# Linear attention scores in three visits of 32x32 matmul tiles instead of seven, from packed copies of K and Q

## The chip, the core and the metric

One core of a Trainium2 chip runs the whole program. The metric is device time in microseconds (us) of that core, the median of several executions of the same program. TensorE (PE) does the matmuls, and its weight loads have a row of their own (PEld); VectorE (DVE) and ScalarE (ACT) work on tiles element by element and can read PSUM, GpSimd (POOL) works element by element on SBUF, and SyncE (SP) issues most DMAs. Each engine runs its own instructions in program order, and engines wait for each other by semaphores.

## The reference, cut to what matters

The program is one layer of a hybrid model: an input projection whose columns feed a gated linear recurrence (group A, 16 column blocks) and an HGRN2 linear attention (group B, 16 heads of 128 channels), then an output projection. There are 512 latent tokens (T) behind 256 context tokens (C), 768 in all (TA). The change concerns the scores of the linear attention:

```python
F = jnp.cumsum(gc, axis=2)
diff = F[:, :, :, None, :] - F[:, :, None, :, :]
decay = jnp.exp(jnp.where(causal[:, :, None], diff, -jnp.inf))
scores = jnp.einsum('bhtk,bhsk,bhtsk->bhts', qc, kc, decay)
o = jnp.einsum('bhts,bhsv->bhtv', scores, vc) + jnp.einsum('bhtk,bhkv->bhtv', qc * jnp.exp(F), s)
```

Every pair of a query t and a key s in a chunk is weighted by the product of the forget factors f between them, channel by channel, forwards and backwards in time. The kernel uses chunks of 128 tokens. In such a chunk the pairs are split by the highest bit in which t and s differ: the diagonal (t = s), and seven levels l = 0 to 6, level l holding the pairs in neighbouring blocks of m = 2^l tokens. At each level K and Q already carry the decay to the edges of their blocks, so that a plain matmul gives the scores of that level.

## The kernel before, in words

The program first computes norms and modulations, then walks the input projection column block by column block. A column block is a *unit*. A unit takes four *slots* (`g` = 0 to 3); in a slot, PE does four K steps of projection matmuls. Each step has three matmuls (high part by high part, high by low, low by high; `mm_unit`) of 512 columns (L177), or of 256 and of 512 columns where the context is needed too (L174, L175). So a slot has 12 matmuls in a unit without context (q and gb), and 24 in a unit with it (ff, v, fb). At the start of each slot ACT rounds the weights for a later slot to a high part `whi` (L127), and POOL subtracts to get the low part `wlo` (L128).

The units of a head come in the order q, gb, ff, v, fb. When fb is done, ACT takes sigmoids, DVE makes the forget factors T (L553) and the keys K (L554), and `steps_b(h)` puts the head's attention work as a list of steps into a queue `wq`. `run_steps` takes steps from it: one at the end of each slot, and one more in the middle of the slot where the next step is marked *fast*. In this way the steps of head h stand, on every engine, between the projection slots of head h+1: the slots of its q and gb units hold `prep` and `level(0)` to `level(6)`, those of ff hold the transposes `ktr` (L526, two of them in a slot) and then the state matmuls `umm` (L654), and so on to `fin`. For the last head, h = 15, the next slots are those of the output projection's first quarter (`q == 0`; 12 matmuls of 512 columns at L826 in each `kb`), where one step runs ahead of each `kb`'s matmuls and where DVE and ACT also split the input y into parts (`y_conv`, L717 and L718).

`prep` packs K into `Kc` on ACT (L563), adds the two directions' K into `kd` (L571) and makes the decayed queries Q (L574, L575). `level(l)` has a PE part and a DVE part. On PE it is a *visit*: 16 matmuls of 32x32 tiles (L581), with 16 more for the diagonal at l = 0 and eight of 64x64 (L609) at l = 6. On DVE it decays K (L613) and Q (L617) to the next block size, merges T (L619), and takes the scores out of PSUM: under a mask into `mc` (copy_predicated, L622) for l < 5, into `mg` for l = 5 and 6 (L631, L635, with ACT's L630 and L634). ACT packs K for the next level after each decay of K (L563), into one of two buffers. The moving operand Q is read in place, in strides.

Among the steps DVE also has the products of the q and gb units (L534, which wait for ACT's sigmoid `sg`, L532) and one accumulation of the output gate in each unit (`gate_step`, L499), until 64 of those are done, which is in head 12. After every 16th of them a step `go` (L506 to L509) is put into the queue, which moves the steps behind it by one slot.

## Time and profile before

| what | before |
| --- | --- |
| median of 3 runs | 2338.56 us (2337.93 to 2340.09) |
| span of the profiled execution | 2338.6 us |
| PE busy | 2254.7 us (96%) |
| DVE busy | 1414.9 us (61%) |
| POOL busy | 931.5 us (40%) |
| ACT busy | 883.7 us (38%) |
| L581, visits of 32x32 tiles: matmuls recorded (two for each of the program's) | 3584 (2560 + 512 + 512) |
| L613, decay of K on DVE | 112, 1579 ns each on average |

The profiled execution has no time of its own beside its span, which is that of the median. Busy times are sums over the whole program, and an engine at 61% may be full in one stage and empty in another; what a stage is bound by is read from the stage. A wait is put down to the engine whose semaphore came last.

### The profile page before, as it was taken

Reading aid. Unit: us, or ns where it says so; the run is one execution under the profiler, and the core shown is the slowest. Engines: PE = TensorE matmul, PEld = TensorE weight load, DVE = VectorE, ACT = ScalarE, POOL = GpSimd, SP = SyncE. Lnnn points to the kernel's source line nnn. Section 1 sums busy time; section 2 is a strip of 40 time slices with the busy share of each in tenths; the row PEclk is TensorE's granted clock in tenths of the full one; section 3 lists DMA queues with packets and bytes.
Section 4 is the critical chain, followed back from the end, with each engine's and each line's share of the span. In section 5 each row is a group of like instructions: output and inputs, shape, how many; then the busy total and the mean of one; then the engine's idle time right before and its main releaser. Section 6 shows DMA issues by size and latency. Waiting matters only on the chain.

```text
span 2338.6 us, 38901 instructions
## 1 busy us (share of the span) xinstructions
PE 2254.7 (96%) x15520; PEld 1863.1 (80%) x15520; DVE 1414.9 (61%) x2223; ACT 883.7 (38%) x1604; POOL 931.5 (40%) x682
## 2 busy tenths in 40 slices
PE   5999999999999999999999999999999998999998
PEld 3568888888888788888788888878878887788886
DVE  4446666666657867766776785686776577720011
ACT  4237677766722232332232222223223223432222
POOL 1225565555533333433333332333333233355552
PEclk9999999999999999999999999999999999999999
DMA  9952222222222222222222232222222123553443
GB/s 342 316 183 78 76 87 82 81 70 93 77 73 77 91 79 84 84 82 84 80 77 86 74 96 77 75 90 82 82 82 77 65 64 105 159 179 95 123 125 108
DMA packets 119086, 241.95 MB, mean 103 GB/s; under 512 B 13556, under 2 KB 13940, under 8 KB 118904
## 3 DMA queue, kind: packets, MB, share of 16 engines
q1 hardware_dynamic: 116216, 231.06, 31.2%
q0 software_dynamic: 2688, 8.40, 0.9%
q8 instruction: 122, 2.00, 0.3%
q14 instruction: 60, 0.49, 0.1%
HBM read 226.81 MB, written 12.59 MB: 102 GB/s over the span
## 4 chain that ended last, share of the span: by engine, by line
PE 61%; DVE 20%; issue 5%; ACT 4%; POOL 1%; ACTq 0%; POOLq 0%; DVEq 0%
PE m L175 22%; PE m L174 11%; PE m L177 8%; PE w L826 8%; PE m L826 6%; DVE ktok L526 5%; DVE KK L613 4%; DVE QQ L617 3%; PE w L654 2%; PE w L352 1%; DVE T L619 1%; DVE mg L631 1%; PE w L351 1%; DVE KK L554 1%; DVE gacc L499 1%
## 5 line engine op out<-in xcount | busy, mean ns | idle before, releaser
L128 POOL TENSOR_TENSOR wlo<-wraw,whi 128x512 fp32r<-128x512 f32 x556 | 784.3, 1415 | 1140.9 <-ACT whi L127 1072.5
L175 PE MATMUL m<-h,whi 128*128 128x512 f32 x1984 | 738.5, 395 | 0.0
L174 PE MATMUL m<-h,whi 128*128 128x256 f32 x1984 | 563.1, 284 | 1.5 <-ACT xp L303 1.5
L127 ACT CAST whi<-wraw 128x512 fp32r<-128x512 f32 x556 | 342.2, 620 | 551.6 <-PE m L175 181.0
L177 PE MATMUL m<-h,whi 128*128 128x512 f32 x1440 | 456.0, 398 | 0.0
L175 PEld LDWEIGHTS m<-h,whi 128*128 128x128 f32 x1984 | 372.3, 188 | 82.6 <-issue 0.7
L175 PE MATMUL m<-h,wlo 128*128 128x512 f32 x992 | 391.1, 394 | 0.0
L174 PEld LDWEIGHTS m<-h,whi 128*128 128x128 f32 x1984 | 375.0, 189 | 4.3 <-ACT xp L303 1.9
L177 PEld LDWEIGHTS m<-h,whi 128*128 128x128 f32 x1440 | 263.4, 188 | 55.0 <-issue 0.5
L177 PE MATMUL m<-h,wlo 128*128 128x512 f32 x720 | 281.3, 391 | 0.0
L174 PE MATMUL m<-h,wlo 128*128 128x256 f32 x992 | 279.0, 281 | 0.0
L175 PEld LDWEIGHTS m<-h,wlo 128*128 128x128 f32 x992 | 186.0, 187 | 44.9
L174 PEld LDWEIGHTS m<-h,wlo 128*128 128x128 f32 x992 | 187.3, 189 | 0.0
L613 DVE TENSOR_TENSOR KK<-KK,T 128x768 f32<-128x768 f32 x112 | 176.8, 1579 | 2.7 <-PE w L609 1.8
L177 PEld LDWEIGHTS m<-h,wlo 128*128 128x128 f32 x720 | 135.2, 188 | 29.8
L320 DVE SCALAR_TENSOR_TENSOR u<-xp,P,u 128x256 f32<-128x256 f32 x96 | 86.5, 960 | 114.4 <-ACT u L318 114.4
L526 DVE STREAM_TRANSPOSE ktok<-KK 32x384 f32<-32x384 f32 x256 | 145.7, 569 | 3.3
L563 ACT COPY Kc<-KK 128x512 f32<-128x512 f32 x80 | 54.8, 684 | 176.2 <-DVE KK L613 119.8
L617 DVE TENSOR_TENSOR QQ<-QQ,T 128x512 f32<-128x512 f32 x112 | 115.3, 1030 | 0.4 <-PE w L581 0.2
L526 DVE STREAM_TRANSPOSE vtok<-ktok 32x192 f32<-32x192 f32 x256 | 94.6, 370 | 13.1 <-ACT ktok L539 9.9
L826 PE MATMUL m<-whi,yh 128*128 128x512 f32 x256 | 102.0, 399 | 0.0
L826 PE MATMUL m<-wlo,yh 128*128 128x512 f32 x256 | 101.2, 395 | 0.0
(209 smaller groups left out, 3068.1 us busy)
## 6 DMA issues: line engine op xcount, KB each, us to landing
wraw<-in_wi SPq DMA_DIRECT2D x428, 256.0 KB, 3.2
araw<-in_adas SPq DMA_DIRECT2D x64, 512.0 KB, 6.1
wraw<-in_wo SPq DMA_DIRECT2D x128, 256.0 KB, 2.6
wraw<-in_adag SPq DMA_DIRECT2D x64, 256.0 KB, 2.7
y_d<-ys POOLq DMA_DIRECT2D x32, 256.0 KB, 2.4
wraw<-y_d SPq DMA_DIRECT2D x32, 256.0 KB, 2.8
h<-in_xT SPq DMA_DIRECT2D x16, 384.0 KB, 7.5
w0raw<-in_w SPq DMA_DIRECT2D x16, 320.0 KB, 6.6
```

The costliest lines, as they stand in the source:

```text
L127: act.copy(hi, t)
L128: pool.tensor_sub(lo, t, hi.bitcast(F32))
L174: pe.matmul(ph[:, 0, 0:C], w, h[:, 0:C], start=s, stop=e)
L175: pe.matmul(ph[:, 1, :], w, h[:, C:TA], start=s, stop=e)
L177: pe.matmul(ph, w, h[:, C:TA], start=s, stop=e)
L320: dve.scalar_tensor_tensor(dst, xp[:, o + k:o + k + n], cw, dst, op0=ALU.mult, op1=ALU.add)
L526: dve.transpose(dst[32 * j:32 * j + 32, :, 32 * i:32 * i + 32], src[32 * i:32 * i + 32, :, 32 * j:32 * j + 32])
L563: act.copy(kc.rearrange("p c n -> p (c n)").rearrange("p (a b c) -> p a b c", b=2, c=m), view(s["K"], C, [[2 * m, C // m], [TA + m, 2], [1 ...
L613: dve.tensor_mul(kk, kk, view(Tm, 1, [[2, nb // 2], [nb - 1, 2], [0, m]]))
L617: dve.tensor_mul(qq, qq, view(Tm, nb + 1 + C // m, [[2, C // m], [-nb - 1, 2], [0, m]]))
L654: pe.matmul(pw[:, i, :], s["kt"][:, 6 * tl[o + i][0] + tl[o + i][1], :], s["v"][:, tl[o + i][1], :], start=True, stop=True)
L826: pe.matmul(pos[tk], y[:, 128 * tk:128 * tk + 128], wlin(x), start=(kb == 0 and n == 0), stop=(kb == 2 * KB - 1 and n == 2))
```

## The change

The two functions `diag` and `level` are taken apart into `kdecay`, `qdecay`, `tmerge`, `scores` and `keep`. The eight steps `prep`, `level(0)` to `level(6)` become eight others, listed in `pairs`: `prep`, the updates of levels 0 and 1, the visit `near` (diagonal and levels 0 to 2 in one PSUM tile) with the update of level 2, the updates of levels 3 and 4, the visit `mid` (levels 3 to 5) with the update of level 5, and the visit `far` (level 6) with the update of level 6. The scores that were taken out of PSUM level by level are taken out after `near` (three copies) and after `mid` (two copies and the `mg` copies). Because levels 0, 1, 3 and 4 are now multiplied after K and Q have been decayed further, their K stays in packed copies (`Kc`, four buffers instead of two) and their Q in new ones (`Qc`, two buffers), which are four more ACT copies a head. The matmul tiles themselves are the same ones. T alternates between two tiles, and the gate accumulator has one buffer instead of two. In the output projection a step marked fast is now followed by another in the same `kb`, if that is fast too.

```diff
-            gst["acc"] = bw.tile([128, 512], F32, name="gacc", bufs=2)
+            gst["acc"] = bw.tile([128, 512], F32, name="gacc", bufs=1)
...
-        def kc_copy(m):
-            kc = bw.tile([128, 4, 128], F32, name="Kc", bufs=2)
-            act.copy(kc.rearrange("p c n -> p (c n)").rearrange("p (a b c) -> p a b c", b=2, c=m),
-                     view(s["K"], C, [[2 * m, C // m], [TA + m, 2], [1, m]]))
-            s["Kc"] = kc
+        def lanes(t, off, m, pitch):
+            return view(t, off, [[2 * m, C // m], [pitch + m, 2], [1, m]])
+
+        def packed(name, src, m, bufs):
+            t = bw.tile([128, 4, 128], F32, name=name, bufs=bufs)
+            act.copy(t.rearrange("p c n -> p (c n)").rearrange("p (a b c) -> p a b c", b=2, c=m), src)
+            return t
+
+        def kc_copy(l):
+            m = 1 << l
+            s["Kc", l] = packed("Kc", lanes(s["K"], C, m, TA), m, 4)
+
+        def qc_copy(l):
+            m = 1 << l
+            s["Qc", l] = packed("Qc", lanes(s["Q"], 0, m, T), m, 2)
 
         def prep():
-            kc_copy(1)
+            kc_copy(0)
...
-        def tiles32(pw, lhs, rhs):
+        def tiles32(pw, o, lhs, rhs):
-                    pe.matmul(pw[32 * j:32 * j + 32, 32 * c:32 * c + 32], lhs(c, j), rhs(c, j), start=True, stop=True)
...
+                    pe.matmul(pw[32 * j:32 * j + 32, o + 32 * c:o + 32 * c + 32], lhs(c, j), rhs(c, j),
+                              start=True, stop=True)
+
+        sl = lambda c, j: slice(128 * c + 32 * j, 128 * c + 32 * j + 32)
+        at = lambda t, c, j: t[:, c, 32 * j:32 * j + 32]
+
+        def kdecay(l):
+            m = 1 << l
+            nb = TA // m
+            kk = view(s["K"], 0, [[2 * m, nb // 2], [TA + m, 2], [1, m]])
+            dve.tensor_mul(kk, kk, view(s["T"], 1, [[2, nb // 2], [nb - 1, 2], [0, m]]))
+
+        def qdecay(l):
+            m = 1 << l
+            nb = TA // m
+            qq = lanes(s["Q"], 0, m, T)
+            dve.tensor_mul(qq, qq, view(s["T"], nb + 1 + C // m, [[2, C // m], [-nb - 1, 2], [0, m]]))
+
+        def tmerge(l):
+            nb = TA >> l
+            t2 = bw.tile([128, 2, nb // 2], F32, name=f"T{1 + l % 2}")
+            dve.tensor_mul(t2.rearrange("p a b -> p (a b)"), view(s["T"], 0, [[2, nb]]), view(s["T"], 1, [[2, nb]]))
+            s["T"] = t2
+
+        def up(l, kc, qc):
+            def go():
+                if qc:
+                    qc_copy(l)
+                kdecay(l)
+                if kc:
+                    kc_copy(l + 1)
+                qdecay(l)
+                tmerge(l)
+            return go
+
+        def scores(ls):
+            pw = psw.tile([128, 4, 128], F32, name="w")
+            s["pw"] = pw
+            wl = pw.rearrange("p a b -> p (a b)")
+            for i, l in enumerate(ls):
+                if l < 0:
+                    tiles32(wl, 128 * i, lambda c, j: s["kd"][:, sl(c, j)], lambda c, j: s["q"][:, sl(c, j)])
+                elif l < 5:
+                    kc, qc = s.pop(("Kc", l)), s.pop(("Qc", l), None)
+                    m = 1 << l
+                    tiles32(wl, 128 * i, lambda c, j: at(kc, c, j),
+                            (lambda c, j: at(qc, c, j)) if qc is not None else
+                            (lambda c, j: view(s["Q"], 128 * c + 32 * j, [[2 * m, 16 // m], [T + m, 2], [1, m]])))
+                else:
+                    K, Q = s["K"], s["Q"]
+                    tiles32(wl, 128 * i, lambda c, j: K[:, j % 2, C + 128 * c + 32 * j:C + 128 * c + 32 * j + 32],
+                            lambda c, j: Q[:, 1 - j % 2, 128 * c + 32 * (j ^ 1):128 * c + 32 * (j ^ 1) + 32])
+
+        def keep(l, r):
+            dve.copy_predicated(s["mc"], MK[:, l, None, :].to_broadcast([128, 4, 32]),
+                                s["pw"][:, r, :].rearrange("p (a b) -> p a b", b=32))
+
+        def near():
+            scores((-1, 0, 1, 2))
+
+        def near_up():
+            kdecay(2)
+            kc_copy(3)
             mc = bw.tile([128, 4, 32], F32, name="mc")
-            act.copy(mc.rearrange("p a b -> p (a b)"), pw[:, 0:128])
+            act.copy(mc.rearrange("p a b -> p (a b)"), s["pw"][:, 0, :])
             s["mc"] = mc
-
...
+            qdecay(2)
+            tmerge(2)
+            for l in range(3):
+                keep(l, l + 1)
+
+        def mid():
+            scores((3, 4, 5))
+
+        def mid_up():
+            kdecay(5)
+            qdecay(5)
+            tmerge(5)
+            keep(3, 0)
+            keep(4, 1)
+            mg = bw.tile([128, 4, 128], F32, name="mg")
+            s["mg"] = mg
+            for j in range(4):
+                r = slice(32 * j, 32 * j + 32)
+                i = j ^ 1
+                act.copy(mg[r, :, 32 * i:32 * i + 32], s["pw"][r, 2, :].rearrange("p (a b) -> p a b", b=32))
+                dve.tensor_copy(mg[r, :, r], s["mc"][r])
+
+        def far():
+            pw = psw.tile([128, 4, 128], F32, name="w")
+            s["pw"] = pw
+            wl = pw.rearrange("p a b -> p (a b)")
+            for c in range(4):
+                for j in range(2):
+                    k0, q0 = C + 128 * c + 64 * j, 128 * c + 64 * (1 - j)
+                    pe.matmul(wl[64 * j:64 * j + 64, 64 * c:64 * c + 64], s["K"][:, j, k0:k0 + 64],
+                              s["Q"][:, 1 - j, q0:q0 + 64], start=True, stop=True)
+
+        def far_up():
+            kdecay(6)
+            qdecay(6)
+            tmerge(6)
+            p4 = s["pw"].rearrange("p a b -> p (a b)")[:, 0:256].rearrange("p (a b) -> p a b", b=64)
+            act.copy(s["mg"][0:64, :, 64:128], p4[0:64])
+            dve.tensor_copy(s["mg"][64:128, :, 0:64], p4[64:128])
+
+        both = lambda f, g: lambda: (f(), g())
+        pairs = [prep, up(0, True, True), up(1, True, True), both(near, near_up), up(3, True, True),
+                 up(4, False, True), both(mid, mid_up), both(far, far_up)]
...
-        return ([prep] + [level(l) for l in range(7)] + [fast(ktr(i)) for i in range(4)] + [umm(0), umm(4), umm(8), omm, otr, fin])
+        return (pairs + [fast(ktr(i)) for i in range(4)] + [umm(0), umm(4), umm(8), omm, otr, fin])
...
                     run_steps(1)
+                    if wq and hasattr(wq[0], "fast"):
+                        run_steps(1)```

What the change does to the order is shown at three places of a middle head. The first is on DVE, from the decay of level 1 to the decay of level 3 (`T_` with a number is one of T's tiles; KK is K, QQ is Q, w is the visit's PSUM tile). Before:

```order
L613 TENSOR_TENSOR KK<-KK,T_14589 128x192x2x2
L617 TENSOR_TENSOR QQ<-QQ,T_14589 128x128x2x2
L619 TENSOR_TENSOR T_14631<-T_14589 128x384
L622 COPY_PREDICATED mc<-MK,w 128x128
L499 SCALAR_TENSOR_TENSOR gacc<-wraw,sc,gacc 128x512
L613 TENSOR_TENSOR KK<-KK,T_14631 128x96x2x4
L617 TENSOR_TENSOR QQ<-QQ,T_14631 128x64x2x4
L619 TENSOR_TENSOR T_14676<-T_14631 128x192
L622 COPY_PREDICATED mc<-MK,w 128x128
L534 TENSOR_TENSOR q<-m,sg 128x512
L613 TENSOR_TENSOR KK<-KK,T_14676 128x48x2x8
```

And now:

```order
L601 TENSOR_TENSOR KK<-KK,T_14585 128x192x2x2
L607 TENSOR_TENSOR QQ<-QQ,T_14585 128x128x2x2
L612 TENSOR_TENSOR T_14611<-T_14585 128x384
L499 SCALAR_TENSOR_TENSOR gacc<-wraw,sc,gacc 128x512
L601 TENSOR_TENSOR KK<-KK,T_14611 128x96x2x4
L607 TENSOR_TENSOR QQ<-QQ,T_14611 128x64x2x4
L612 TENSOR_TENSOR T_14705<-T_14611 128x192
L645 COPY_PREDICATED mc<-MK,w 128x128 x3
L534 TENSOR_TENSOR q<-m,sg 128x512
L601 TENSOR_TENSOR KK<-KK,T_14705 128x48x2x8
```

DVE's instructions are the same ones; the copies of levels 0, 1 and 2 stand together behind the merge of level 2.

The second place is ACT, in the same slots of the head and on to the `mg` copies of level 5. Before:

```order
L563 COPY Kc<-KK 128x512
L127 CAST whi<-wraw 128x512
L563 COPY Kc<-KK 128x512
L532 ACTIVATE sg<-m 128x512
L127 CAST whi<-wraw 128x512
L563 COPY Kc<-KK 128x512
L127 CAST whi<-wraw 128x512 x2
L630 COPY mg<-w 32x4x32 x4
```

And now:

```order
L127 CAST whi<-wraw 128x512
L566 COPY Kc<-KK 128x512
L655 COPY mc<-w 128x128
L532 ACTIVATE sg<-m 128x512
L127 CAST whi<-wraw 128x512
L566 COPY Qc<-QQ 128x512
L566 COPY Kc<-KK 128x512
L127 CAST whi<-wraw 128x512
L566 COPY Qc<-QQ 128x512
L127 CAST whi<-wraw 128x512
L676 COPY mg<-w 32x4x32 x4
```

The copy `mc` of the diagonal has moved from the first visit to a place just ahead of the sigmoid of the q unit, and the copies `Qc` of levels 3 and 4 stand between the casts of the weights.

The third place is DVE from the decay of level 4 to the decay of level 6. Before:

```order
L613 TENSOR_TENSOR KK<-KK,T_14723 128x24x2x16
L617 TENSOR_TENSOR QQ<-QQ,T_14723 128x16x2x16
L619 TENSOR_TENSOR T_14763<-T_14723 128x48
L622 COPY_PREDICATED mc<-MK,w 128x128
L613 TENSOR_TENSOR KK<-KK,T_14763 128x12x2x32
L617 TENSOR_TENSOR QQ<-QQ,T_14763 128x8x2x32
L619 TENSOR_TENSOR T_14803<-T_14763 128x24
L631 COPY mg<-mc 32x4x32 x4
```

And now:

```order
L601 TENSOR_TENSOR KK<-KK,T_14739 128x24x2x16
L607 TENSOR_TENSOR QQ<-QQ,T_14739 128x16x2x16
L612 TENSOR_TENSOR T_14763<-T_14739 128x48
L601 TENSOR_TENSOR KK<-KK,T_14763 128x12x2x32
L607 TENSOR_TENSOR QQ<-QQ,T_14763 128x8x2x32
L612 TENSOR_TENSOR T_14834<-T_14763 128x24
L645 COPY_PREDICATED mc<-MK,w 128x128 x2
L677 COPY mg<-mc 32x4x32 x4
```

The copies of levels 3 and 4 now stand behind the merge of level 5, ahead of the `mg` copies, and the decay of K of level 5 (the fourth row) follows a merge of T and no copy.

## Rows read from the trace of the kernel before

**Rows 1.** The page, engines' busy time and share, and the chain that ended last
```profile
PE 2254.7 (96%) x15520; PEld 1863.1 (80%) x15520; DVE 1414.9 (61%) x2223; ACT 883.7 (38%) x1604; POOL 931.5 (40%) x682
...
PE 61%; DVE 20%; issue 5%; ACT 4%; POOL 1%; ACTq 0%; POOLq 0%; DVEq 0%
```

**Rows 2.** Stretches: us, busy time (instructions) of each engine, granted clock, DMA share, GB/s
```profile
1534.46:1575.08 40.62, 38.65 (x404) 30.45 (x403) 40.09 (x56) 12.03 (x24) 16.29 (x11) 1.00 0.27 85
1788.73:1827.49 38.76, 38.47 (x404) 30.45 (x403) 37.84 (x54) 12.13 (x24) 16.40 (x11) 1.00 0.23 76
945.16:988.35 43.19, 43.19 (x430) 34.54 (x429) 39.31 (x57) 12.67 (x25) 19.38 (x13) 1.00 0.28 86
1953.83:2002.44 48.61, 38.92 (x380) 29.50 (x379) 43.06 (x64) 19.13 (x37) 16.94 (x13) 0.96 0.42 131
...
2002.20:2005.50 3.30, 2.92 (x11) 2.76 (x12) 1.43 (x4) 0.27 (x1) 0.00 (x0) 0.50 0.60 164
```

**Rows 3.** PE's waits: line and releaser, us in total, times, longest
```profile
PE w L654 <- DVE ktok L526: 17.7, 14, 3.3
PE w L581 <- ACT Kc L563: 7.5, 16, 0.9
PE w L581 <- DVE T L619: 5.5, 11, 0.5
```

**Rows 4.** PE in order of time, one head: start us, us, instruction, xcount
```profile
1538.93 0.46 PE L581 MATMUL w<-q,kd 128*32 128x32 f32 x32
1539.20 0.56 PE L581 MATMUL w<-QQ,Kc 128*32 128x32 f32 x32
1539.69 0.72 PE L177 MATMUL m<-h,whi 128*128 128x512 f32 x2
...
1545.67 0.39 PE L177 MATMUL m<-h,wlo 128*128 128x512 f32 x1
1545.99 0.46 PE L581 MATMUL w<-QQ,Kc 128*32 128x32 f32 x32
1546.38 0.73 PE L177 MATMUL m<-h,whi 128*128 128x512 f32 x2
1546.94 0.40 PE L177 MATMUL m<-h,wlo 128*128 128x512 f32 x1
...
1547.64 0.39 PE L177 MATMUL m<-h,wlo 128*128 128x512 f32 x1
```

**Rows 5.** DVE in order of time, the same head
```profile
1553.81 0.94 DVE L613 TENSOR_TENSOR KK<-KK,T 128x768 f32<-128x768 f32 x1
1554.68 1.78 DVE L617 TENSOR_TENSOR QQ<-QQ,T 128x512 f32<-128x512 f32 x1
1556.38 1.29 DVE L619 TENSOR_TENSOR T<-T 128x48 f32<-128x48 f32 x1
1557.60 0.28 DVE L622 COPY_PREDICATED mc<-MK,w 128x128 f32<-128x128 uint8 x1
...
1558.66 0.68 DVE L617 TENSOR_TENSOR QQ<-QQ,T 128x512 f32<-128x512 f32 x1
1559.27 0.17 DVE L619 TENSOR_TENSOR T<-T 128x24 f32<-128x24 f32 x1
1559.36 1.91 DVE L631 COPY mg<-mc 32x128 f32<-32x128 f32 x4
```

**Rows 6.** POOL in order of time, the same head
```profile
1554.24 3.36 POOL L128 TENSOR_TENSOR wlo<-wraw,whi 128x512 fp32r<-128x512 f32 x2 [2.14 <-PE w L581]
```

**Rows 7.** ACT in order of time, the same head
```profile
1539.46 0.27 ACT L589 COPY mc<-w 128x128 f32<-128x128 f32 x1 [1.32 <-PE w L581]
...
1549.12 0.62 ACT L563 COPY Kc<-KK 128x512 f32<-128x512 f32 x1 [2.76 <-DVE KK L613]
```

**Rows 8.** Groups of instructions: count, busy us, mean ns, idle before: the split of y
```profile
L718 DVE TENSOR_TENSOR yl<-wraw,yh 128x512 fp32r<-128x512 f32 x32 | 40.1, 1257 | 28.7 <-ACT yh L717 28.5
```

**Rows 9.** PE in order of time, last head, in the output projection
```profile
2002.58 1.84 PE L654 MATMUL w<-vtok,ktok 128*128 128x128 f32 x7 [3.35 <-DVE ktok L526]
```

More of the change, by code (lines that the diff above doesn't have):

```diff
@@ L576, in prep @@
             s["Q"] = Q
-        def tiles32(pw, lhs, rhs):
+        def tiles32(pw, o, lhs, rhs):
             for c in range(4):
                 for j in range(4):
-                    pe.matmul(pw[32 * j:32 * j + 32, 32 * c:32 * c + 32], lhs(c, j), rhs(c, j), start=True, stop=True)
-        def diag():
-            pw = psw.tile([128, 512], F32, name="w")
-            kd, q = s["kd"], s["q"]
-            sl = lambda c, j: slice(128 * c + 32 * j, 128 * c + 32 * j + 32)
-            tiles32(pw, lambda c, j: kd[:, sl(c, j)], lambda c, j: q[:, sl(c, j)])
+                    pe.matmul(pw[32 * j:32 * j + 32, o + 32 * c:o + 32 * c + 32], lhs(c, j), rhs(c, j),
+                              start=True, stop=True)
@@ L838, in layer_kernel @@
                     run_steps(1)
+                    if wq and hasattr(wq[0], "fast"):
+                        run_steps(1)
                 elif op is None:
```

45 lines of the change are left out of this document (removed).

## The prediction

> **What bounds the kernel now.** I read the page first. PE is busy for 96% of the span, which suggests that every visit taken off PE is worth its length; but the chain that ended last gives PE only 61% and DVE 20%, although DVE is busy for 61% of the whole [rows 1]. So there are stretches in which PE is not what ends last. The waits of PE say where: at `umm(0)` it waits for DVE's transposes `ktr` in 14 of 16 heads, 17.7 us in all, and at the visits for Kc and T, 7.5 and 5.5 us [rows 3]. Then I cut one head into two stretches, from the first DVE instruction after the fb unit to the end of `ktr`, and from there to the next fb unit. In the first, which holds all visits, DVE works 40.09 of 40.62 us, the rest being gaps between instructions [rows 2]. DVE does nothing there but work through its list, and PE, which has to wait for the end of the list at `umm(0)`, has time to spare. This stretch holds every matmul that the change touches. In the second stretch PE sets the pace, and nothing of it is changed. The length of a head is therefore the length of DVE's list plus the second stretch, and a head gets shorter only where DVE's list does.
>
> **What PE saves.** A triple of projection matmuls takes 0.70 us (1546.94 to 1547.64), and the one that holds a one-group visit 1.27 (1545.67 to 1546.94), so such a visit costs 0.57 us [rows 4]. From its first tile to the next projection matmul it takes 0.39 us (1545.99 to 1546.38), and the visit with two groups 0.76 (1538.93 to 1539.69), so a second group with Q in strides costs 0.37; the diagonal, with packed operands, takes 0.27 (1538.93 to 1539.20) [rows 4]. Before, the visits of the diagonal and levels 0 to 5 cost 6 x 0.57 + 0.37 = 3.79 us a head. Now `near` costs 0.57 + 3 x 0.27 and `mid` 0.57 + 2 x 0.27, in sum 2.49; `far` is as it was. PE saves 1.3 us a head, 21 us in 16 heads. In the heads where DVE's list is the limit it doesn't get to the end of the program: PE reaches `umm(0)` earlier and waits longer. I book 0. Nor do PE's waits at the visits (13 us) come free, since they are for DVE's results, directly or by an ACT copy.
>
> The Trainium skill ("TensorEngine Tiling (Array Packing)", Key Properties) says that a change of tiling mode drains TensorE. The row agrees, with about 0.3 us of 0.57 that is not tiles, and by that rule alone the kernel would gain those 21 us; it is a rival below.
>
> **What changes in DVE's list.** By the order, DVE has the same instructions. Four things can lengthen or shorten it.
>
> First, the place of the five masked copies (0.28 us each, about 0.20 of which adds to the list, since each begins before the one ahead has ended: 1557.60 to 1557.79) [rows 5]. Where a copy stood in front of an instruction that was held up anyway, it cost nothing before. DVE's products are held up by POOL's subtractions: the same decay of Q takes 0.68 us, but 1.78 while POOL subtracts; T's merge takes 0.17 (of a tile of 24 columns), but 1.29 (of 48); the four `mg` copies 1.91 [rows 5, 6]. So a subtraction costs DVE 1.1 us, wherever it meets the list, and one stands in each slot. The copy of level 0 was hidden in this way, those of levels 1, 2 and 4 were not. Now all of levels 3 and 4 come after the merge of level 5, 0.4 us, and three stand together after the merge of level 2, 0.6 us, where they are followed by the product q, which waits for ACT's `sg` in any case.
>
> Second, ACT's copy `mc` now stands after a Kc copy and ahead of `sg` and the next cast. The first masked copy waits for it: a Kc copy takes 0.62 us and `mc` 0.27 [rows 7], 0.9 after the decay of K, while DVE has the decay of Q and a merge to do, 0.8. That is 0.1 us. `sg`, the cast and with it POOL's subtraction are 0.15 later, and so is the product behind it.
>
> Third, DVE waits for the four Qc copies. A Qc copy of levels 0, 1 and 3 is ready before it is wanted, because the decay of K (0.94) stands ahead. That of level 4 stands behind a Kc copy and a cast on ACT, 3 x 0.62 = 1.9 us after the decay of K of level 3, and is wanted 0.7 + 0.1 + 0.9 = 1.7 after it. Those 0.2 us fall into the time in which POOL's two subtractions hold up the decay of Q anyway (1554.24 to 1557.60) [rows 5, 6]. Booked at 0; 0.25 if this cover is gone.
>
> Fourth, the decay of K of level 5 must wait for the end of `mid`, whose last group waits for the decay of Q just ahead. On PE that is some 0.15 us to start, 0.27 for the tiles, and 0.2 to the end: about 0.6, of which an unhindered merge of T covers 0.1. It costs 0 while POOL holds the merge up (1.29), as it does now, and 0.5 if not [rows 5]. Queued behind that decay are the `mg` copies, the decays of level 6 and all of `ktr`. The decay of Q of level 2 waits for `near`, but there the accumulation `gacc` and a decay of K lie between, over 1.5 us, against some 0.8. The one buffer of `gacc` is free long before it is wanted. Both are booked at 0.
>
> Sum of a head in which DVE is the limit: +0.15 (the later `sg`), then -0.2 - 0.1 for copies no longer ahead of the decays of levels 4 and 5, then +0.4 for the copies after the merge of level 5: between 0 and +0.5, and I take **+0.3**. There are 11 such heads with gate accumulations: +3.3 us.
>
> The others: two heads have the gate's step among the visits, and PE doesn't wait at `umm(0)`; in the one at 945 PE is busy throughout, 43.19 of 43.19, DVE for 39.31 [rows 2]. There PE's saving counts, up to 1.3 us, until DVE's list ends last; part of its 3.9 us of idle time is for the gate's row, which stays. I take -0.5 each, -1.0. The two heads without accumulations have DVE busy 37.84 of 38.76 us [rows 2]; what they save of the idle 0.9, of which gaps are about half, they lose to the later copies: 0.
>
> The last head, in the output projection: 48.61 us, PE busy for 38.92, DVE for 43.06 [rows 2]. With two fast steps in a `kb`, `umm(0)` comes after 10 of them instead of 12, and 2 x 4 x 0.70 = 5.6 us of projection move behind it. DVE's list before it is shorter by two splits of y, 2 x 1.26 = 2.5 [rows 8], and of its idle 5.5 us, which are waits for ACT behind PE, between nothing and all goes. That makes +3.1 to -2.4, and I take +1: the later merges and visits are still waited for.
>
> Sum: 3.3 - 1.0 + 0 + 1 = +3.3. The profiled span, 2338.6 us, is the median, so I predict **2342 us**, in its own range from 2337 to 2347 (11 heads from 0 to +0.5, the last head from -2.4 to +3.1).
>
> **The rivals.**
>
> *A subtraction gets hidden.* POOL runs one in each slot, and the list is held up by eight or so. If one of them in each of the 11 heads now falls under work that doesn't hold it up, the head gains 1.1 us, 12 in all, from the forecast: 2330. For it: the three masked copies in a row last 0.6 us and DVE's short waits add to that; against it: casts and subtractions follow the same ACT order and come within 0.3 us of where they came. [...]
>
> *PE is the bound after all.* Then its 21 us come out: 2338.6 - 21 = 2318. Against it stands DVE's 40.09 of 40.62 us [rows 2].
>
> *The new waits are not covered.* This is the slower side: if the subtractions move so that the merge of level 4 runs free, DVE stands still behind `mid` for 0.5 us, and behind Qc for 0.25, and the copies are hidden nowhere, 0.2 more. Close to 1 us in 13 heads on top of the forecast: 2354. It decides from the point at which `mid`'s end comes later than the end of that merge.
>
> *TensorE's clock.* After the wait of 3.35 us at the last head's `umm(0)` the clock was granted at 0.50, the lower of its two levels, for 3.3 us [rows 2, 9]; after the waits of 1.2 in other heads it was 1.00. PE's waits grow to about 2 us at `umm(0)`. If that is enough, a head loses half of 3.3 us behind it, 18 us in 11 heads: 2360.
>
> That the visits don't get cheaper on PE would change nothing, because PE has time to spare.
>
> **How the numbers follow.** Forecast 0.55, hidden subtraction 0.14, PE the bound 0.05, uncovered waits 0.20, clock 0.06. The range runs from 2330 to 2354, the ends of the first and third rivals, and leaves out the second and the fourth and a part beyond the ends, 2 in 10. A measurement of this kernel can tell 0.2%, 4.7 us, from no change: 2333.9 to 2343.2. The forecast lies within for 0.40 of its 0.55, above it for 0.13 and below for 0.02. Faster 0.21, same 0.40, slower 0.39.
>
> **What would show it.** After the change DVE's stretch from the fb unit to the end of `ktr` should be 40.6 to 41.1 us in a middle head; PE's wait at `umm(0)` should grow from 1.2 to about 2 us, and visits to `near` and `mid` should wait around 1 us for Kc, Qc or Q. In the last head PE should wait over 5 us at `umm(0)`. The forecast is wrong if DVE's stretch gets shorter by more than 0.5 us, or shows idle time of over 0.3 us before the decay of K of level 5.

## The result, and the profile after

The changed kernel takes 2363.19 us (median of 4, 2361.12 to 2369.32) beside 2338.81 for the kernel before: ratio 1.0107, with a 95% interval of 1.0093 to 1.0121. It is 24.4 us slower. The forecast of 2342 was slower too, but by 3 us only, and the range ended at 2354.

The page of the kernel after, busy time and the chain that ended last, answers [rows 1]:

```profile
PE 2247.3 (95%) x15520; PEld 1872.4 (79%) x15520; DVE 1421.6 (60%) x2223; ACT 921.9 (39%) x1668; POOL 940.6 (40%) x682
...
PE 57%; DVE 25%; ACT 4%; issue 4%; POOL 2%; ACTq 0%; DVEq 0%; POOLq 0%
```

PE's share of the chain fell from 61% to 57% and DVE's rose from 20% to 25%. PE's waits (line and releaser, us in total, times, longest) answer [rows 3]:

```profile
PE w L717 <- DVE ktok L526: 36.2, 15, 6.5
...
PE w L591 <- DVE QQ L607: 14.5, 13, 3.0
PE w L591 <- ACT Kc L566: 10.2, 16, 2.3
```

The wait at `umm(0)` doubled, from 17.7 to 36.2 us, and the visits wait longer as well. PE has the fewer visits, and has got more waiting for them. Stretches of the kernel after, with the columns of [rows 2]: a middle head (head 8) from the fb unit to the end of `ktr`; the second stretch, from the end of `ktr` to the next head's first DVE instruction, of heads 10 and 11; 3.4 us behind `umm(0)` of head 10; and the last head:

```profile
1374.02:1415.33 41.31, 37.35 (x404) 30.60 (x402) 40.47 (x56) 14.46 (x28) 16.97 (x11) 1.00 0.27 84
1586.79:1632.61 45.82, 45.76 (x265) 40.39 (x266) 20.42 (x52) 12.25 (x29) 12.23 (x10) 0.96 0.23 75
1673.92:1718.25 44.33, 44.27 (x265) 39.03 (x266) 20.46 (x53) 12.25 (x29) 12.24 (x10) 1.00 0.24 79
...
1587.61:1591.02 3.41, 3.41 (x14) 3.02 (x13) 2.31 (x4) 0.78 (x2) 1.28 (x1) 0.50 0.00 0
1968.86:2017.44 48.58, 34.47 (x356) 27.01 (x355) 41.79 (x62) 19.34 (x37) 15.24 (x11) 0.86 0.38 115
```

DVE still fills the first stretch of a head (40.47 of 41.31 us), which is 0.7 longer than in [rows 2], while PE's busy time in it fell by 1.3 (38.65 to 37.35). The second stretch has grown too in most heads, although none of its work is changed; in heads 10 and 11 of the kernel before it was:

```profile
1575.08:1618.92 43.84, 43.70 (x265) 38.99 (x266) 20.45 (x51) 12.23 (x29) 12.51 (x10) 1.00 0.27 79
1659.55:1703.39 43.84, 43.70 (x265) 38.99 (x266) 20.45 (x51) 12.24 (x29) 12.50 (x10) 1.00 0.25 79
```

The same 265 recorded matmuls take 2.0 us longer in head 10, where the clock was granted at 0.50 for a while, and 0.5 longer in head 11, where it was 1.00 throughout. In head 8 they do not (43.85 before, 43.79 after). I cut both profiled executions at the same places, the first DVE instruction after a head's fb unit and PE's first `umm(0)` matmul:

| stretch, us | before | after | difference |
| --- | --- | --- | --- |
| up to head 0's first stretch | 692.0 | 689.9 | -2.1 |
| 15 heads, fb unit to `umm(0)` | 613.9 | 619.7 | +5.8 |
| 15 heads, `umm(0)` to the next fb unit | 648.0 | 659.3 | +11.3 |
| last head, to `umm(0)` | 48.75 | 48.63 | -0.1 |
| from there to the end | 336.0 | 341.8 | +5.8 |
| span | 2338.6 | 2359.2 | +20.7 |

The first row is not the change's: over all profiled runs of the kernels here, of either kind, it lies between 688.8 and 693.0. So there are three places to explain: the list of DVE, the second stretch, and the output projection. The profiled execution of after took 2361.17 us, 2.0 less than the median; two of the other three took 2365.22 and 2369.32, at mean granted clocks of 0.990 and 0.988 instead of 0.991. The 1.7 us of the 24.4 that are left lie in the profiled execution of before, which was slower than its median (see "The base" below).

### The profile page after: what moved, and what is told of

Its sections match the earlier page's. It is cut to its first block, busy times and chain, and to the rows that moved or that the text cites. A ratio compares the mean times of both kernels' runs of the same rounds, so it can differ in the third digit from the quotient of the medians.

```text
span 2359.2 us, 38833 instructions
## 1 busy us (share of the span) xinstructions
PE 2247.3 (95%) x15520; PEld 1872.4 (79%) x15520; DVE 1421.6 (60%) x2223; ACT 921.9 (39%) x1668; POOL 940.6 (40%) x682
## 4 chain that ended last, share of the span: by engine, by line
PE 57%; DVE 25%; ACT 4%; issue 4%; POOL 2%; ACTq 0%; DVEq 0%; POOLq 0%
PE m L175 22%; PE m L174 11%; PE w L889 7%; DVE KK L601 7%; PE m L889 6%; DVE ktok L526 5%; PE m L177 4%; DVE QQ L607 4%; DVE T L612 2%; PE w L717 2%; PE w L352 1%; DVE KK L554 1%; POOL wlo L128 1%; DVE mc L645 1%; ACT whi L127 1%
## 5 line engine op out<-in xcount | busy, mean ns | idle before, releaser
L128 POOL TENSOR_TENSOR wlo<-wraw,whi 128x512 fp32r<-128x512 f32 x556 | 793.2, 1433 | 1155.1 <-ACT whi L127 1093.9
L127 ACT CAST whi<-wraw 128x512 fp32r<-128x512 f32 x556 | 343.5, 620 | 532.9 <-PE m L175 182.8
L177 PE MATMUL m<-h,whi 128*128 128x512 f32 x1440 | 447.9, 392 | 0.0
L177 PEld LDWEIGHTS m<-h,whi 128*128 128x128 f32 x1440 | 268.1, 188 | 55.3 <-issue 0.5
L177 PE MATMUL m<-h,wlo 128*128 128x512 f32 x720 | 280.7, 390 | 0.0
L601 DVE TENSOR_TENSOR KK<-KK,T 128x768 f32<-128x768 f32 x112 | 175.0, 1563 | 4.9
L177 PEld LDWEIGHTS m<-h,wlo 128*128 128x128 f32 x720 | 135.2, 188 | 28.8
L526 DVE STREAM_TRANSPOSE ktok<-KK 32x384 f32<-32x384 f32 x256 | 145.7, 569 | 3.3
L607 DVE TENSOR_TENSOR QQ<-QQ,T 128x512 f32<-128x512 f32 x112 | 117.3, 1048 | 0.0
L566 ACT COPY Kc<-KK 128x512 f32<-128x512 f32 x80 | 54.8, 685 | 155.0 <-DVE KK L601 126.5
L526 DVE STREAM_TRANSPOSE vtok<-ktok 32x192 f32<-32x192 f32 x256 | 94.5, 369 | 13.1 <-ACT ktok L539 9.9
L724 DVE SCALAR_TENSOR_TENSOR S<-S,T,w 128x128 f32<-128x128 f32 x128 | 44.5, 348 | 96.0 <-PE w L717 61.4
```

The lines of the kernel that those rows point to most:

```text
L127: act.copy(hi, t)
L128: pool.tensor_sub(lo, t, hi.bitcast(F32))
L177: pe.matmul(ph, w, h[:, C:TA], start=s, stop=e)
L526: dve.transpose(dst[32 * j:32 * j + 32, :, 32 * i:32 * i + 32], src[32 * i:32 * i + 32, :, 32 * j:32 * j + 32])
L566: act.copy(t.rearrange("p c n -> p (c n)").rearrange("p (a b c) -> p a b c", b=2, c=m), src)
L601: dve.tensor_mul(kk, kk, view(s["T"], 1, [[2, nb // 2], [nb - 1, 2], [0, m]]))
```

## The experiments

The theory after the result was: the last head pays for its second fast step, DVE's list pays for where the masked copies stand, and in the second stretch TensorE's clock drops behind the longer wait at `umm(0)`. The rival for each is that the three visits themselves cost the time.

### The second fast step

e2_double puts only the second fast step into the kernel before, e1_single takes only that out of the kernel after:

```diff
                     run_steps(1)
+                    if wq and hasattr(wq[0], "fast"):
+                        run_steps(1)
```

> The kernel before with only the second fast step added in the output projection. If that step alone costs, the run is 3 to 6 us slower than before, 2342 to 2345, with the longer stretch behind umm(0) of the last head (some 341 us instead of 336). If its cost comes only together with the three visits, the time stays at 2339.

> The changed kernel with one step a kb in the output projection again. The traces give the stretch from umm(0) of the last head to the end 341.8 us after the change and 336.0 before, while the last head takes 48.6 us up to umm(0) in both. If the second fast step is what costs there, because two kb of projection (5.4 us) have moved behind the wait without shortening it, the run is 4 to 7 us faster than the changed kernel, near 2357, and PE's wait at the last umm(0) falls from 6.5 us to under 4. If the visits near and mid are what delays the last head, the time stays within 2 us of the changed kernel's.

e2_double took 2342.61 us (2340.31 to 2344.95), ratio 1.0017 [1.0007, 1.0026]; e1_single 2358.66 (2355.88 to 2361.46), ratio 1.0086 [1.0069, 1.0103]. The second fast step costs 4.1 us alone (the interval reaches from 1.6 to 6.1) and 4.5 beside the rest. PE at the last head's `umm(0)`, first in e2_double, then in the kernel after (us of start, us):

```profile
2000.20 2.04 PE L654 MATMUL w<-vtok,ktok 128*128 128x128 f32 x8 [6.43 <-DVE ktok L526]
```

```profile
2017.49 2.08 PE L717 MATMUL w<-vtok,ktok 128*128 128x128 f32 x8 [6.50 <-DVE ktok L526]
```

In [rows 9] that wait was 3.35. In e2_double the part behind `umm(0)` grew by 6.5 us, and the part ahead of it got only 1.6 shorter (48.7 to 47.1): two `kb` of projection, 5.6 us, were taken from the place where they covered DVE's list. The rest of the 6.5 is about what the clock took: it was granted at 0.50 around the end of the longer wait, for 6.8 us with 5.07 us of PE's work in them, against 3.4 with 2.97 before. The two stretches, e2_double first, with the columns of [rows 2]:

```profile
1998.44:2005.27 6.83, 5.07 (x16) 4.42 (x17) 3.33 (x7) 0.27 (x1) 0.00 (x0) 0.50 0.28 77
```

```profile
2002.14:2005.55 3.41, 2.97 (x11) 2.81 (x12) 1.54 (x4) 0.27 (x1) 0.00 (x0) 0.50 0.60 163
```

### DVE's list

DVE in order of time in the kernel after, in the head at 1374.02, which answers [rows 5], and POOL and ACT in the same stretch:

```profile
1395.88 1.28 DVE L612 TENSOR_TENSOR T<-T 128x48 f32<-128x48 f32 x1
1397.26 0.96 DVE L601 TENSOR_TENSOR KK<-KK,T 128x768 f32<-128x768 f32 x1
...
1398.83 0.63 DVE L645 COPY_PREDICATED mc<-MK,w 128x128 f32<-128x128 uint8 x2
1399.49 0.91 DVE L677 COPY mg<-mc 32x128 f32<-32x128 f32 x4
...
1401.98 1.79 DVE L607 TENSOR_TENSOR QQ<-QQ,T 128x512 f32<-128x512 f32 x1
1403.69 1.26 DVE L612 TENSOR_TENSOR T<-T 128x12 f32<-128x12 f32 x1
```

```profile
1401.34 4.83 POOL L128 TENSOR_TENSOR wlo<-wraw,whi 128x512 fp32r<-128x512 f32 x3 [4.25 <-ACT whi L127]
...
1399.55 1.07 ACT L676 COPY mg<-w 32x128 f32<-32x128 f32 x4 [4.90 <-DVE mc L645]
```

Set beside the head of [rows 5], counted from its first DVE instruction: the merge of level 4 ends 0.08 us earlier than before; the two masked copies add 0.66; the four `mg` copies take 0.91 where they took 1.91, because POOL is not subtracting; then the decay of Q of level 6 and its merge meet a subtraction both, 1.79 and 1.26, where before only the first did (1.77, and 0.16 for the merge). That is -0.08 + 0.66 - 1.0 + 1.1 = +0.68, the 0.7 by which the stretch grew. The subtraction that left the `mg` copies did not fall under anything, it came back at the last merge. ACT's row suggests why it moved: its `mg` copies, which read the PSUM tile that DVE's masked copies read, wait for those now (`mc`), the casts queued behind them are late, and three subtractions stand in a row.

Four kernels tell apart what of this costs. e11_nokeep34 and e12_nokeep012 leave the masked copies of levels 3 and 4, and of levels 0 to 2, out of e1_single (those scores are missing from the result):

```diff
-            keep(3, 0)
-            keep(4, 1)
```

> The changed kernel with one step a kb in the output projection (2358.7 us, list of a middle head 41.3) without the two masked copies of levels 3 and 4: their scores are left out. In the trace these two copies take 0.66 us from the merge of level 5 to the first mg copy. If they are what makes the list longer than before (40.6), the list falls by 0.6 to 0.7 us, to 40.6 or 40.7, and the run is 7 to 12 us faster, 2347 to 2352. If POOL's subtractions take the room, it stays within 0.2 us of 41.3 or moves by a whole subtraction, 1.1.

```diff
-            for l in range(3):
-                keep(l, l + 1)
```

> The same kernel (2358.7 us, list 41.3) without the three masked copies of levels 0, 1 and 2 instead: their scores are left out. In the trace of the run with spread copies, taking them from this place only exposed DVE's wait for sg and moved POOL's subtraction into the decay of K behind it, which ended at the same time. So these three should cost the list nothing: it stays at 41.1 to 41.4 us and the time within 4 us of 2358.7. If copies cost by their number alone, the list falls by 1.0 us and the time by 13.

e11_nokeep34 took 2348.15 us (2347.59 to 2352.16), ratio 1.004 [1.0025, 1.0055], 10.5 less than e1_single; e12_nokeep012 2358.3 (2355.11 to 2361.04), ratio 1.0075 [1.0059, 1.0092], no less, though the lower clock (below) came in seven of its heads, against three. A middle head of e11_nokeep34, with the columns of [rows 2]:

```profile
1368.63:1409.23 40.60, 37.41 (x404) 30.62 (x403) 39.82 (x54) 14.49 (x28) 17.16 (x11) 1.00 0.29 85
```

It is 0.7 shorter without the two copies behind level 5, which over the 15 heads is 8.0 us (619.5 to 611.5); without the three behind level 2 the list is what it was (41.3), since the product q behind them waits 0.48 us for `sg` then. So two of the five copies account for the whole growth of the list. That it is their place and not the copies as such is argued from the kernel before, which has the same two in a list of 40.6.

e4_actfirst issues ACT's `mg` copies ahead of the two masked copies, so that the casts aren't late; e10_spread does that in e1_single and also spreads all masked copies singly among the products of levels 3 and 5:

```diff
-            keep(3, 0)
-            keep(4, 1)
             mg = bw.tile([128, 4, 128], F32, name="mg")
...
                 act.copy(mg[r, :, 32 * i:32 * i + 32], s["pw"][r, 2, :].rearrange("p (a b) -> p a b", b=32))
+            keep(3, 0)
+            keep(4, 1)
+            for j in range(4):
+                r = slice(32 * j, 32 * j + 32)
                 dve.tensor_copy(mg[r, :, r], s["mc"][r])
```

> The changed kernel with ACT's four mg copies of level 5 issued ahead of the two masked copies on DVE, which read the same PSUM tile. In the changed kernel ACT waits 5 us a head there for DVE (80 us in 16 heads), and the cast behind it is 2.4 us late. If that delay pushes one more of POOL's subtractions into DVE's list, the list of a middle head shrinks from 41.3 to about 40.3 us and the run is 10 to 15 us faster, near 2350. If the list is longer only because the masked copies stand in runs (0.34 us each instead of 0.20) and because decays that wait for another engine start 0.1 us later, ACT's wait goes but list and time stay within 3 us.

```diff
                 kdecay(l)
+                if kp:
+                    keep(0, 1)
...
                 qdecay(l)
+                if kp:
+                    keep(1, 2)
...
+            kdecay(5)
+            keep(3, 0)
+            qdecay(5)
+            keep(4, 1)
+            tmerge(5)
```

> The changed kernel with one step a kb in the output projection (2358.7 us), and the five masked copies no longer in runs of three and two: one each between the decays and merges of level 3, and of level 5 (ACT's mg copies ahead of them). If runs of masked copies (0.34 us each against 0.20) and the decays that start 0.1 us after a wait make the list 0.7 us longer, the list of a middle head falls from 41.3 to 40.5 to 40.8 us and the run is 6 to 10 us faster, 2349 to 2353. If the list is longer for another reason (the place of POOL's subtractions), it stays within 0.2 us and the time within 3.

e4_actfirst took 2364.48 us (2361.21 to 2366.86), ratio 1.0106 [1.0091, 1.0121], with a list of 41.3: nothing gained. Its casts came in time, but DVE met the two subtractions all the same, now at the merge of level 5 (1.26) and at the accumulation `gacc` (1.82, and 0.75 in the kernel before):

```profile
1399.68 1.26 DVE L612 TENSOR_TENSOR T<-T 128x24 f32<-128x24 f32 x1
...
1402.47 1.82 DVE L499 SCALAR_TENSOR_TENSOR gacc<-wraw,sc,gacc 128x512 f32<-128x512 f32 x1
```

So the late casts are not the cause of the longer list, as I had thought on seeing them; by e11_nokeep34 the two copies are. e10_spread took 2364.91 (2363.74 to 2365.69), ratio 1.0107 [1.0092, 1.0122], which is slower than e1_single and missed its expectation: its list is 41.8 us. DVE's rows in one of its heads say why:

```profile
1392.60 0.69 DVE L534 TENSOR_TENSOR q<-m,sg 128x512 f32<-128x512 f32 x1 [0.47 <-ACT sg L532]
...
1400.21 0.20 DVE L612 TENSOR_TENSOR T<-T 128x48 f32<-128x48 f32 x1
1400.88 0.96 DVE L601 TENSOR_TENSOR KK<-KK,T 128x768 f32<-128x768 f32 x1 [0.47 <-PE w L591]
```

The three copies had filled the wait for `sg`, which is now idle time of 0.47, and the decay of K of level 5 now stands still behind `mid` for 0.47. That second wait is the one that the prediction priced at 0.5 us if uncovered, and it appears under the condition that its third rival named: the merge of level 4 ahead of it runs free, 0.20 us where it took 1.28.

### The clock

In the kernel after, the clock was granted at 0.50 for 3.4 us right at `umm(0)` in heads 0, 4, 7 and 10, in the row at 1587.61 above, with PE busy all through it: 1.7 us are lost. Behind those the second stretch took 45.1 to 45.8 us, and 43.7 to 44.3 in other heads (apart from 3, 6, 9 and 12, which have the gate's own steps). In the former PE had waited 2.44 to 2.47 us just before, and in seven of the others it had too. Other kernels with waits of 2.40 to 2.48 us in the same 11 heads show the lower clock there in three (e1_single), five (e4_actfirst) and seven (e12_nokeep012), e11_nokeep34 with waits of 1.77 us in two; the kernel before, with 1.2, in none. e3_fill and e9_fill2 put idle matmuls (their result isn't used) into that wait, five of them in the kernel after, two in e1_single (and other numbers in the heads with another wait):

```diff
+                nf = {3: 1, 6: 0, 13: 0, 14: 0, 15: 3}.get(h, 2) if o == 0 else 0
+                if nf:
+                    pf = psw.tile([128, 512], F32, name="w")
+                    for _ in range(nf):
+                        pe.matmul(pf, ones, s["q"], start=True, stop=True)
```

> The changed kernel with idle fp32 matmuls (ones by q, 512 columns, results unread) put ahead of umm(0): five in most heads, some 2.2 us, thirteen in the last, so that PE works where it waited for 2.4 and 6.5 us. If the waits at umm(0) make the clock fall now and then (four heads of 16 in the profiled run, about 2 us each, and the last head), no middle head shows the half clock behind umm(0) and the run is 6 to 12 us faster than the changed kernel, 2351 to 2357, with less spread between runs. If the half clock comes from something else, it stays, and the time is the same or up to 5 us slower for the added work.

> The changed kernel with one step a kb in the output projection (2358.7 us) and fewer idle matmuls ahead of umm(0) than in the run with five: two in most heads (0.9 us each in that run's trace, 1.8 us, against a wait of 2.4), three in the last. If the wait at umm(0) is what lets the clock fall, no middle head shows the half clock, the lists stay at 41.3 us since the idle matmuls end ahead of them, and the run is 4 to 9 us faster, 2350 to 2355. If the five idle matmuls kept the clock up only because they made PE the bound, the half clock comes back in some heads and the time stays near 2358.

e3_fill took 2378.5 us (2377.7 to 2379.18), ratio 1.0167 [1.0152, 1.0182], and missed: I had the idle matmuls too short. PE in one of its heads, just ahead of `umm(0)`:

```profile
1421.62 4.45 PE L719 MATMUL w<-q,ones 128*128 128x512 f32 x10
```

Five of them (ten records) take 4.45 us, 2 more than the wait, and set the pace. But no middle head had the lower clock. With two, e9_fill2 took 2352.15 us (2349.93 to 2354.86), ratio 1.0056 [1.004, 1.0073], 6.5 less than e1_single with more work on PE. The middle of the program (705 to 1945 us, some fourteen heads) of e9_fill2, and of the kernel after:

```profile
705.00:1945.00 1240.00, 1209.92 (x9789) 1026.61 (x9789) 879.79 (x1562) 387.28 (x820) 430.42 (x310) 1.00 0.26 79
```

```profile
705.00:1945.00 1240.00, 1191.27 (x9710) 1018.29 (x9709) 875.20 (x1545) 386.51 (x817) 428.05 (x308) 0.99 0.24 79
```

The list did not change (41.3), the wait left over is 0.8 us, and the second stretches fell by 6.1 us (658.7 to 652.6). All four executions of e9_fill2 have a mean granted clock of 0.995 to 0.997, those of e1_single 0.991 to 0.993. So the lower clock behind `umm(0)` comes with the idle time there, and it costs 6 to 7 us.

### Where the three visits pay

If the saving on PE is lost only because DVE's list is full, it must come out where the list is shorter. e5_before_gate and e6_after_gate move the gate's accumulations out of the visits' slots into those of the v and fb units, in the kernel before and in e1_single:

```diff
-        gate_raw(i + 1)
...
-        elif u >= NA + 5 and g == 2 and gi < 4 * KB:
-            if gi == 0:
-                gate_raw(0)
-            gate_step(gi)
-            gi += 1
+        elif (4 * (u - NA) + g) % 20 in (10, 12, 14, 16, 18) and g != 3:
+            p = (4 * (u - NA) + g) % 20
+            if p > 10:
+                gate_step(gi)
+                gi += 1
+            if p < 18:
+                gate_raw(gi)
```

> The kernel before with the gate's accumulations moved: four in the slots of each head's v and fb units instead of one in each unit, so that none stands in DVE's list between the fb unit and the end of ktr. If DVE's list is the bound there, the list gets 1.3 us shorter in 11 heads (two accumulations of 0.67), PE's wait of 1.2 us at umm(0) goes to about 0, and the run is 10 to 15 us faster than before, 2324 to 2329. If PE is the bound, it stays at 2339.

> The changed kernel with one step a kb in the output projection (2358.7 us) and the gate's accumulations moved in the same way. PE has 2.4 us of wait at umm(0) here, so the whole 1.3 us of the list should count in 13 heads, 17 us: 2340 to 2344, with a wait at umm(0) of 1.1 us and fewer stretches of half clock. If PE's idle time isn't behind DVE's list alone, less than 10 us comes out.

e5_before_gate took 2322.65 us (2321.68 to 2324.09), ratio 0.9927 [0.9912, 0.9942]; e6_after_gate 2317.73 (2317.47 to 2318.07), ratio 0.9906 [0.9891, 0.992]. The sign has turned: with the gate out of the list the kernel with three visits is 5 us ahead. The expectation of e6_after_gate, 2340 to 2344, was missed by 22 us. The list fell by 3.0 us (41.3 to 38.3), more than the two accumulations (1.3), because two collisions with POOL went as well, as its rows show:

```profile
1366.14 0.97 DVE L644 COPY_PREDICATED mc<-MK,w 128x128 f32<-128x128 uint8 x3
1367.01 0.68 DVE L533 TENSOR_TENSOR q<-m,sg 128x512 f32<-128x512 f32 x1
1367.61 0.95 DVE L600 TENSOR_TENSOR KK<-KK,T 128x768 f32<-128x768 f32 x1
...
1377.45 0.68 DVE L606 TENSOR_TENSOR QQ<-QQ,T 128x512 f32<-128x512 f32 x1
1378.06 1.26 DVE L611 TENSOR_TENSOR T<-T 128x12 f32<-128x12 f32 x1
```

```profile
1366.14 1.30 POOL L128 TENSOR_TENSOR wlo<-wraw,whi 128x512 fp32r<-128x512 f32 x1 [0.75 <-ACT whi L127]
```

The decay of K of level 3 takes 0.95 where it took 1.68 in the kernel after, and the decay of Q of level 6 0.68 where it took 1.79. One subtraction lies entirely under the three masked copies and the product q, and none of the four is held up. It is still the list that separates this pair, and not yet what PE saves: a head of e5_before_gate, then of e6_after_gate, with the columns of [rows 2]; PE waits 0.5 and 0.6 us at `umm(0)` in them.

```profile
1355.69:1394.54 38.85, 38.47 (x404) 30.47 (x403) 37.97 (x54) 12.13 (x24) 16.43 (x11) 1.00 0.25 76
```

```profile
1351.43:1389.70 38.27, 37.23 (x404) 30.54 (x403) 37.33 (x54) 14.52 (x28) 16.89 (x11) 1.00 0.26 77
```

e7_before_late and e8_after_late go on from these two: DVE's five `mg` copies, and in e8_after_late the masked copies of levels 3 and 4 too, are issued behind `umm(0)`, where DVE has time:

```diff
+                if o == 0:
+                    s["pw"] = s["pm"]
+                    keep(3, 0)
+                    keep(4, 1)
+                    for j in range(4):
+                        r = slice(32 * j, 32 * j + 32)
+                        dve.tensor_copy(s["mg"][r, :, r], s["mc"][r])
+                    dve.tensor_copy(s["mg"][64:128, :, 0:64], s["p4"][64:128])
```

> The kernel before with the gate's accumulations moved (2322.7 us) and with DVE's five copies into mg (1.3 us a head) behind the state matmuls of umm(0), so that they too leave the list. With the accumulations moved PE waits only 0.5 us a head at umm(0). If PE with its seven visits becomes the bound there, only that comes out, 8 us: 2313 to 2317, with no wait at umm(0) left. If DVE's list were still the only bound, all 1.3 us in 15 heads would, 20 us: 2303.

> The changed kernel with one step a kb in the output projection and the gate's accumulations moved (2317.7 us), and with the masked copies of levels 3 and 4 and DVE's five copies into mg behind the state matmuls of umm(0): 2.0 us a head leave the list. If the three visits have freed PE, as the trace of before gave it (1.3 us a head), PE follows the shorter list further than in the kernel with seven visits: 0.8 to 1.5 us in 15 heads, 2295 to 2306, at least 8 us under the other kernel of this pair. If PE's waits inside near and mid hold it, the two kernels of the pair end within 4 us of each other.

e7_before_late took 2310.26 us (2308.28 to 2312.43), ratio 0.9877 [0.9862, 0.9891]; e8_after_late 2301.39 (2300.26 to 2303.16), ratio 0.984 [0.9823, 0.9856], the fastest here. One middle head of e7_before_late, then of e8_after_late, with the columns of [rows 2]:

```profile
1347.49:1385.68 38.19, 38.19 (x404) 30.45 (x403) 35.55 (x49) 12.12 (x24) 16.31 (x11) 1.00 0.25 77
```

```profile
1341.50:1378.96 37.46, 36.88 (x404) 30.51 (x402) 36.60 (x47) 14.52 (x28) 16.79 (x11) 1.00 0.24 78
```

With seven visits PE is now busy for all 38.19 us and ends last, and DVE waits for it, 1.88 us at the visit of level 6 alone; so it does not matter here that e7_before_late leaves its masked copies in the list. With three visits PE needs 36.88, 1.3 less, as worked out in the prediction, and ends last as well, after 0.58 us of waiting for Kc at `near` and none at `umm(0)`. The difference is 0.73 us a head, 11 in 15 heads, of which 9 appear in the time. The three visits do save on PE what they promise, in a kernel whose DVE leaves PE nothing to wait for at `umm(0)`; of the 1.3 us a head, 0.6 go into the wait at `near`.

## Why the prediction was wrong

**Where the error lies.** On the span the forecast was +3.3 us and the traces give +20.7, of which -2.1 stand ahead of head 0. The largest part is a step that booked nothing: "In the second stretch PE sets the pace, and nothing of it is changed." Those stretches grew by 11.3 us, some 7 of them by the lower clock behind the longer wait at `umm(0)` (e9_fill2 takes it away), the rest without a cause found. Then come the last head with what follows it, -0.1 + 5.8 = +5.7 against +1, and DVE's list with +5.8 against +2.3. The signs that the prediction named for itself nearly all came about (the wait at `umm(0)` at 2.4 us, the one of the last head over 5, the list at 41.3, 0.2 beyond its bound), so they could not show what was left out: they look at DVE's list and at waits, and none at the second stretch.

**What held.** DVE's list is the limit of a middle head. PE's 21 us, booked at 0, went into the wait at `umm(0)`, from 1.2 to 2.44 us ("about 2"). The Qc copies cost nothing; the decay of K of level 5 stood 0.1 us behind `mid`, under a merge of T that POOL held up. The three copies behind level 2 are hidden. The two heads without accumulations gained 0.5 and 0.6 us, against 0.

PE at `near` and `mid` in the same head shows the costs and waits that the prediction named for the visits:

```profile
1383.88 0.46 PE L591 MATMUL w<-q,kd 128*32 128x32 f32 x32
1384.15 0.76 PE L591 MATMUL w<-Qc,Kc 128*32 128x32 f32 x64
1385.46 0.46 PE L591 MATMUL w<-QQ,Kc 128*32 128x32 f32 x32 [0.55 <-ACT Kc L566]
...
1396.01 0.46 PE L591 MATMUL w<-QQ,KK 128*32 128x32 f32 x32 [1.01 <-DVE QQ L607]
```

**"I take +1" for the last head.** It and what follows it measured +5.7 in the trace, beyond the upper end of +3.1. The second fast step alone costs 4.1 to 4.5 of that, and the visits alone another 2 (e1_single: 50.7 us to `umm(0)` against 48.75, 336.2 behind it against 336.0). The step that failed is "of its idle 5.5 us, which are waits for ACT behind PE, between nothing and all goes". None went: with the second fast step alone DVE's idle time there is 5.9 us (e2_double), with the visits alone 6.9 (e1_single), with both 6.8 (48.58 less 41.79). Taking the projection away did not shorten these waits. The last head of e1_single also had a granted clock of 0.90, against 0.96 in [rows 2]; how much of the 2 us is the clock's no run tells.

**"+0.4 for the copies after the merge of level 5", and a head "+0.3".** It was +0.68 in the middle head (+0.6 up to `umm(0)`) and 5.8 us in all against 3.3 - 1.0 + 0. I took 0.20 for a copy from single ones; two in a row take 0.33 each. The +0.15 and the -0.3 "for copies no longer ahead" came as -0.08 together. And the subtraction that I counted as fixed moved from the `mg` copies to the last merge, at +0.1 on balance. The two heads with the gate's step, booked at -0.5 each, came as +0.8 and -0.4.

**The rival with 0.06.** "If that is enough" was the question that it put on the wait of 2 us at `umm(0)`, and the answer is: sometimes. Of 11 heads with a wait of 2.4 us the clock fell in 4 in the profiled run, and in 3 to 7 in those of its variants. That it cost "half of 3.3 us" was right (1.7), so the rival was worth 6 to 7 us and not 18. The prediction saw the wait grow and priced it as free time in the forecast and in the range.

**The base.** The forecast put the change on the profiled span as if that were a time. A time lies 1.8 to 2 us above the span of the same execution (2361.17 over 2359.2), so the profiled execution of before stood for some 2340.5, 1.7 above the median.

**What stays open.** Of the 11.3 us in the second stretches some 4 are not the lower clock. In that of head 11, shown above, the granted clock is 1.00, PE is busy for 44.27 of 44.33 us, and the same matmuls took 43.70 before. Counted from `umm(0)`, kernels built from the change show 44.1 to 44.3 in some heads, also e8_after_late (44.1 in four), which doesn't wait at `umm(0)`; those built from the kernel before show 43.6 to 43.7, but for heads with the gate's own steps. In heads 2, 5 and 11 a matmul of 512 columns is followed by the next one after 233 to 241 ns on average, against 230 to 232 in head 1 and in the kernel before; what holds them back no run here tells. Nor do the runs tell why the clock falls in one head and not in the next after the same wait.

## What to carry to other kernels

Before an engine is relieved, see which engine's list ends the stage; if it is another one, the relief becomes a wait, and a wait of TensorE can cost clock, so it isn't free. Then first shorten the list that ends last (here by moving DVE's accumulations and copies to a stretch in which it has time, 28 us in the kernel with seven visits), and the same three visits pay 9 us instead of costing 20 (e1_single). Where work is grouped, ask for each piece what it stood in front of before, a wait that hid it or a neighbour that didn't.

## What the runs showed of the hardware

- A collision of DVE with one of POOL's subtractions cost 1.0 to 1.1 us at decays, merges, the accumulation and the `mg` copies alike, and less in places: 0.7 at the decay of K of level 3 in the kernel after (1.68 against 0.95). Masked copies out of PSUM are not held up: three took 0.97 us under a subtraction (1366.14 above) and 0.98 without one. A plain copy from SBUF is held up, though it has one input: the longest `mg` copy before took 1297 ns, the median 219.
- The Trainium skill ("SBUF — State Buffer", Who interferes with whom) says of plain copies that they can enter a mode with both port pairs and then contend with GpSimd; the 1297 ns agree with that.
- ACT's and DVE's copies out of one PSUM tile went one after the other in this program: ACT's `mg` copies ended a wait of 4.90 us when DVE's masked copies of another part of the tile were done (1399.55 above).
- One idle matmul of 128x512 elements, in fp32 throughout, took 0.89 us (4.45 for five), against 0.23 for one of the projection's (0.70 for three, [rows 4]).
